# Reordering ScalarE's and VectorE's steps inside the seven-product pairs, and masking attention scores by one more product

## The chip, the cores and the metric

The kernel runs on one core of one Trainium2 chip. The metric is device time: microseconds (us) from the launch to the end on that core, lower is better. TensorE (PE) multiplies, VectorE (DVE), ScalarE (ACT) and GpSimd (POOL) work on tiles in the on-chip memory, SyncE (SP) issues most transfers, and POOL issues those that add into their target.

## What is computed

One inference step of a two-layer encoder for 512 prompt frames and 64 sample frames. The model width is 1024. Layer 0 mixes frames with gated DeltaNet and a short convolution, layer 1 with stick-breaking attention (16 heads of 64); each layer has a SwiGLU feed-forward block (FFN) before and after its mixer. The text counts them in order: FFN 0, mixer 0, FFN 1, FFN 2, mixer 1, FFN 3.

```python
def _swiglu(h, w_in, w_out):                       # D_FF = 2816
    gate, up = jnp.split(h @ w_in, 2, axis=-1)
    return (jax.nn.silu(gate) * up) @ w_out

def _sb_block(q, k, v, q_pos, k_pos):              # stick-breaking attention
    z = jnp.einsum('hqd,hkd->hqk', q, k) * SB_DH ** -0.5
    visible = k_pos[None, :] < q_pos[:, None]
    log_rest = jnp.where(visible, -jax.nn.softplus(z), 0.0)
    later = lax.cumsum(log_rest, axis=2, reverse=True) - log_rest
    w = jnp.where(visible, jnp.exp(jax.nn.log_sigmoid(z) + later), 0.0)
    return jnp.einsum('hqk,hkd->hqd', w, v)

for l in range(DEPTH):                             # DEPTH = 2
    mod = (silu(c) @ ada_w[l] + ada_b[l]) ...      # shift, scale, gate of each sub-layer
    x = x + 0.5 * gate[0] * _swiglu(modulated_norm(x), ff_w_in[l, 0], ff_w_out[l, 0])
    x = x + gate[1] * (delta_and_conv_mixer if l == 0 else stick_breaking_mixer)(modulated_norm(x))
    x = x + 0.5 * gate[2] * _swiglu(modulated_norm(x), ff_w_in[l, 1], ff_w_out[l, 1])
y = _rmsnorm(x, final_g)
```

## The kernel before

All 576 frames are the moving side of every projection, in two halves of 288 columns; weights come in as tiles of 128x128. Every operand is split into a high and a low part (names with H and L, or wh and wl), and one exact product is three matmuls: high by high, low by high, high by low. Such a projection matmul of 288 columns has the tile name `d` as its output, or `a` in one of the seven products, and is called dense below.

The weights are cut into *pairs* of two column tiles, each in two *granules* of 512 KB. `w_dma` (line 370) loads a granule into one of three `stage` buffers. `w_prep` and `w_split` make wh by a copy on ACT and wl by a subtraction on DVE or POOL; where `by_dma` is set (the flag `S2M`, on in FFN 0 to 2), ACT writes the negated high part into wl and a transfer issued on POOL adds the stage tile to it (`acc_dma`).

**Seven-product pairs.** 67 of the input pairs of the four FFNs run through `dense7` (line 514): a 2x2 block product done with seven block products instead of eight, named in the order in which they run P1, P2, P6, P5, P7, P3, P4. Each is 4 blocks of 3 matmuls, so a pair is 84 dense matmuls where a plain one is 96. The weight side needs four sums (`w_sum` 1 to 4, on DVE, tiles `ss`) and four split tiles (`w_tile` 0 to 3). Tile 0 is the stage granule itself, tiles 1 and 2 are sums, and tile 3 is a half tile (`wh3`, `wl3`) that the last product uses. The products share three banks of the accumulation memory: P1, P6, P7 and P4 go through one bank, P5 and P3 through another. So ACT's copy of P1 out of its bank has to be done before P6 may add to it, that of P6 before P7, and so on. `evac7` (line 820) takes the products out: ACT copies (`sg`, `hm`, `up`), DVE sums, and then the split of the result into HH and HL. That last part of a pair (`late`: the product with the gate, HH, HL) runs after the following pair has begun.

**Mixer 1.** Twelve pairs project q, k and v, and the output projection follows. Eight attention tasks (`att_pair`, line 1484; two heads each) are put between the dense matmuls. A task has nine steps. Step i of a task is `scores(i)`: three matmuls of 64 to 512 columns; two sigmoids on ACT (`sg`, `sn`); three operations on POOL that force the last 64 columns of `sg` and `sn` to 0 and 1 where a key is not visible; a running product on DVE from the right (`cp`); a product on DVE (`sg`). Then `transp` turns `sg` round on PE, copies it to `wt`, and after steps 3, 7 and 8 `pv` multiplies it with v. Before its steps a task loads the cached keys and values through SP (`ck`, `vc`) and stores its new k and v the same way.

**Mixer 0** works in the same way with convolutions (`conv_task`, in `raw` buffers handed out by `raw_tile`), small inverses and the recurrence over chunks. **Ada tiles** (`ada_task`) are vector products for shift, scale and gate (`jk<-aw`, two operations on DVE each), spread over the FFNs and mixer 1.

**What sets the order.** The program is unrolled in Python: for each instruction a small model of the engines' clocks (`Model`) adds a cost, and the planner `Sched` decides after each dense block (`S.tick`) whether a task is due. The compiler keeps this order on each engine. So an edit that changes the model's clocks moves instructions elsewhere too. An engine runs its list strictly in order, and SP's loads wait in the list for their buffers.

The evacuation steps of `dense7` are driven by these lines of the main loop:

```python
if n == 0: ... w_tile(i, 3)                       # half tile of this pair, right after P1
k = {0: 0, 3: 1, 5: 2}.get(n)                      # tile 0 after P1, tile 1 after P5, tile 2 after P3
```

Of the kernel before, what the change touches and what calls it, by code (L numbers as in the profile page):

```python
# [303 lines left out]
def encoder_step(ctx: ExitStack, tc: tile.TileContext, a, o):  # L304
# [61 lines left out]
    nxt = [0]  # L366
    share = [False]
# [20 lines left out]

    def w_split(i, src, E=V, by_dma=False):
        n = Model.size(src)  # L390
        if n == HB:
            h, l = (wsp.tile([P, HB], F32R, name=m, bufs=1) for m in ("wh3", "wl3"))
        else:
            h, l = wsp.tile([P, 1024], F32R, name="wh"), wsp.tile([P, 1024], F32R, name="wl")
        wt.setdefault(i, []).append((h, l))
        for c in range(0, n, HB):
            A.activation(h[:, c:c + HB], src[:, c:c + HB], AF.Copy)
        if by_dma:
            A.activation(l[:, :n], src, AF.Copy, scale=-1.0)
            acc_dma(l[:, :n].bitcast(F32), src)  # L400
            return
        E.tensor_sub(l[:, :n], src, h[:, :n].bitcast(F32))

# [16 lines left out]
    def w_tile(i, n):  # L420

        if n == 0:
            w_split(i, st[i, 0], by_dma=S2M[0])
        if n == 1:
            w_split(i, ss[i, 1])
        if n == 2:
            w_split(i, ss.pop((i, 3)))
            ss.pop((i, 1))
            st.pop((i, 0))
            w_dma()  # L430
        if n == 3:
            w_split(i, st[i, 1][:, HB:], by_dma=S2M[0])
            st.pop((i, 1))
            w_dma()

    def w_prep(i, g, E=None):
        if i >= len(pairs) or g >= len(pairs[i]):
            return
        if seven(i):
            if g == 0:  # L440
                w_sum(i, 1)
                w_tile(i, 0)
                w_sum(i, 2)
            else:
                w_sum(i, 3)
                w_tile(i, 1)
# [5 lines left out]
        A.activation(h[:, :n], s[:, :n], AF.Copy)  # L452
        E = E or G if E or share[0] and M.t["POOL"] + 1.1 * n < M.t["DVE"] else V
# [60 lines left out]
    def dense7(evac):  # L514
# [12 lines left out]
        for n, (name, u, xf) in enumerate(order):  # L527
# [15 lines left out]
            if n == 0:  # L543
                if len(wt[i]) < 3:
                    w_sum(i, 4)
                    w_tile(i, 2)
                w_tile(i, 3)
            if nxt7:
                for k in {1: (1,), 2: (2,), 4: (3, 4)}.get(n, ()):
                    w_sum(i + 1, k)  # L550
                k = {0: 0, 3: 1, 5: 2}.get(n)
                if k is not None:
                    w_tile(i + 1, k)
            elif n in (2, 4):
                w_prep(i + 1, n // 2 - 1)
        if not nxt7:
            for n in (0, 1, 2):
# [257 lines left out]
    def ffn(l, s, pool, task, out):  # L815
# [5 lines left out]
        def evac7(jj):  # L821
# [4 lines left out]
            def products(ps):  # L826
                hm = {}

                def mul():
                    for half in (1, 0):  # L830
                        hm[half] = pool.tile([P, 288], F32, name="hm", bufs=2)
                        V.tensor_mul(hm[half], g[half], up[1] if half else ps)

                def high():
                    for half in (1, 0):
                        A.activation(HHc[:, jj, t0s[half]:t0s[half] + 288], hm[half], AF.Copy)

                def low():
                    for half in (1, 0):
                        r = slice(t0s[half], t0s[half] + 288)  # L840
                        V.tensor_sub(HLc[:, jj, r], hm[half], HHc[:, jj, r].bitcast(F32))
                late.update({0: mul, 1: high, 2: low})
# [6 lines left out]
            def evac(step, ps):  # L849
                if step == "P1":  # L850
                    g[0] = copy("sg", ps, 3)
                n = {"P1": 0, "P2": 1, "P6": 2}.get(step, step)
                if step == "P6":
                    g[1] = copy("sg", ps, 3)
                if n in late:
                    late.pop(n)()
                if step == "P2":
                    V.tensor_add(g[0], g[0], ps)
                if step == "P5":
                    up[0] = copy("hm", ps, 2)  # L860
# [11 lines left out]
        for ci, (j0, nj) in enumerate(CHUNKS):  # L872
            HH = pool.tile([P, 8, NT], F32R, name="HH")
            HL = pool.tile([P, 8, NT], F32R, name="HL")
            for jj in range(nj):
                gate = {}

                def evac(g, half, ps, jj=jj, gate=gate):
# [4 lines left out]
                    else:  # L883
                        h = pool.tile([P, 288], F32, name="hm", bufs=2)
# [27 lines left out]
    def mixer0(pool, task, npool):  # L912
# [78 lines left out]
        def conv_task(c, i, raw, out):  # L991
            w = sm["w_qkv"][:, {"q": 0, "k": 4, "v": 8}[c] + i]
            for j in range(4):
# [6 lines left out]
                yield S.clock  # L1000
            yield M.ready(out)
            A.activation(out, out, AF.Silu)

        def raw_tile():
            S.until(lambda: sum(not t[2] for t in convs) < 3)
            return pool.tile([P, RAW], F32, name="raw", bufs=4)
# [66 lines left out]
        def gdn_pair(p, kq, vt):  # L1073
# [50 lines left out]
            for n in range(4):  # L1124
                T.transpose(pv[:, n, :], vt[:, n * P:(n + 1) * P], ident)
# [748 lines left out]
```

## Time and profile before

| what | value |
|---|---|
| median of the runs (lowest to highest) | 2476.76 us (2473.92 to 2480.23) |
| the profiled execution, its own time | 2483.51 us |
| span, first to last instruction | 2481.5 us |
| mean granted clock of TensorE | 0.970 of full speed |
| PE busy | 2353.2 us (95%) |
| DVE busy | 1783.9 us (72%) |
| ACT busy | 1142.1 us (46%) |
| POOL busy | 487.2 us (20%) |
| mean traffic | 133 GB/s |

The busy shares are averages over stages with different limits, and PE's busy time counts overlapping matmuls at their pipelined length. The six stages, in us from the start of the span: FFN 0 0 to 474, mixer 0 to 879, FFN 1 to 1291, FFN 2 to 1701, mixer 1 to 2036, FFN 3 to the end. In the rows below, `a<-b,c` is the tile written and the tiles read, `x` a count, and what stands behind `<-` at an idle time is the engine and tile that ended it.

### The profile page before, as it was taken

What the parts mean: (1) busy time and instruction counts of PE and PEld (TensorE: products, weight loads), DVE (VectorE), ACT (ScalarE), POOL (GpSimd) and SP (SyncE); (2) the same over time, 40 slices, a digit from 0 to 9 for tenths busy, and PEclk for the clock granted to TensorE, in tenths of its full rate; (3) what the DMA queues carried; (4) which work ended last, traced back from release to release, by engine and by line L of the source; (5) the groups of instructions that cost most, each with busy time, mean ns of one, the idle gap of its engine ahead of it and who ended that gap; (6) DMA issues with size and microseconds to landing.
All of it is one profiled execution on the core that took longest, in us unless ns stands there. A gap on an engine that the chain in (4) does not pass through costs nothing. (4 is left out here: it accounts for less than half of the span.)

```text
span 2481.5 us, 46116 instructions
## 1 busy us (share of the span) xinstructions
PE 2353.2 (95%) x18280; PEld 2262.4 (91%) x18280; DVE 1783.9 (72%) x3491; ACT 1142.1 (46%) x2297; POOL 487.2 (20%) x723
## 2 busy tenths in 40 slices
PE   7989899999989999999999999999999979999998
PEld 5989899988878989999999999999888869999998
DVE  7788977587886678686867656466777767848475
ACT  4434626453322355372644446364555445426352
POOL 4100101342231230010132001013443334000001
PEclk9999999998888999999999999999999979999999
DMA  6666757231123156485736556353343315423222
GB/s 242 188 201 191 212 174 179 86 109 53 54 59 98 54 160 189 146 215 160 198 123 179 157 122 159 97 145 100 121 147 115 106 66 140 131 77 102 87 85 82
DMA packets 113115, 329.45 MB, mean 133 GB/s; under 512 B 26706, under 2 KB 29010, under 8 KB 112644
## 3 DMA queue, kind: packets, MB, share of 16 engines
q1 hardware_dynamic: 95044, 273.02, 32.8%
q0 software_dynamic: 17856, 53.49, 12.7%
q8 instruction: 144, 2.36, 0.4%
q14 instruction: 71, 0.58, 0.1%
HBM read 261.47 MB, written 11.51 MB: 110 GB/s over the span
## 5 line engine op out<-in xcount | busy, mean ns | idle before, releaser
L191 PE MATMUL d<-XH,wh 128*128 128x288 f32 x2280 | 702.2, 308 | 17.5 <-ACT XH L191 8.3
L191 PE MATMUL d<-XL,wh 128*128 128x288 f32 x2280 | 687.0, 301 | 15.0 <-POOL XL L191 11.6
L191 PE MATMUL d<-XH,wl 128*128 128x288 f32 x2280 | 686.4, 301 | 9.5 <-DMA wl<-stage 7.9
L191 PEld LDWEIGHTS d<-XH,wh 128*128 128x128 f32 x2280 | 438.8, 192 | 32.2 <-ACT XH L191 14.6
L191 PEld LDWEIGHTS d<-XL,wh 128*128 128x128 f32 x2280 | 439.1, 193 | 22.7 <-POOL XL L191 18.1
L191 PEld LDWEIGHTS d<-XH,wl 128*128 128x128 f32 x2280 | 439.0, 193 | 13.7 <-DMA wl<-stage 11.7
L191 ACT ACTIVATE wh<-stage 128x512 fp32r<-128x512 f32 (+3 forms) x412 | 325.8, 817 | 225.3 <-PE d L191 215.9
L191 PE MATMUL d<-HH,wh 128*128 128x288 f32 x1408 | 416.7, 296 | 1.0 <-ACT HH L191 1.0
L191 PE MATMUL d<-HL,wh 128*128 128x288 f32 x1408 | 416.3, 296 | 0.3
L191 PE MATMUL d<-HH,wl 128*128 128x288 f32 x1408 | 414.2, 294 | 0.0
L191 DVE TENSOR_TENSOR wl<-stage,wh 128x1024 fp32r<-128x1024 f32 (+3 forms) x219 | 246.5, 1133 | 125.6 <-ACT wh L191 123.7
L191 PE MATMUL d<-TH,wh 128*128 128x288 f32 x1072 | 319.9, 298 | 15.3 <-ACT sg L191 12.3
L191 DVE SCALAR_TENSOR_TENSOR jk<-aw,cb 128x1024 fp8e4<-128x1024 f32 x256 | 315.9, 1234 | 4.4
L191 PE MATMUL d<-TL,wh 128*128 128x288 f32 x1072 | 316.3, 295 | 0.0
L191 PE MATMUL d<-TH,wl 128*128 128x288 f32 x1072 | 316.1, 295 | 0.0
L191 DVE SCALAR_TENSOR_TENSOR x<-d,mod,x 128x64 f32<-128x64 f32 (+2 forms) x384 | 146.4, 412 | 225.0 <-PE d L191 224.1
L191 PEld LDWEIGHTS d<-HL,wh 128*128 128x128 f32 x1408 | 264.3, 188 | 1.7 <-DVE HL L191 1.7
L191 PEld LDWEIGHTS d<-HH,wh 128*128 128x128 f32 x1408 | 264.2, 188 | 1.4 <-ACT HH L191 1.4
L191 PEld LDWEIGHTS d<-HH,wl 128*128 128x128 f32 x1408 | 264.6, 188 | 0.0
L563 POOL DMA_DIRECT2D wl<-stage x100 | 86.7, 867 | 847.5 <-ACT wl L191 357.3
L191 ACT ACTIVATE wh<-ss 128x512 fp32r<-128x512 f32 x268 | 158.2, 627 | 153.8 <-DVE ss L191 153.4
L191 PEld LDWEIGHTS d<-TH,wh 128*128 128x128 f32 x1072 | 201.2, 188 | 24.8 <-ACT sg L191 19.7
(325 smaller groups left out, 3796.8 us busy)
## 6 DMA issues: line engine op xcount, KB each, us to landing
stage<-in_w SPq DMA_DIRECT2D x301, 512.0 KB, 3.8
aw<-in_ada SPq DMA_DIRECT2D x128, 512.0 KB, 4.4
wl<-stage POOLq DMA_DIRECT2D x50, 512.0 KB, 5.4
stage<-in_w SPq DMA_DIRECT2D x36, 384.0 KB, 3.1
wl<-stage POOLq DMA_DIRECT2D x50, 256.0 KB, 3.3
TL<-XL POOLq DMA_DIRECT2D x8, 576.0 KB, 8.4
TL<-ss POOLq DMA_DIRECT2D x8, 576.0 KB, 6.7
TL<-in_ada SPq DMA_DIRECT2D x8, 512.0 KB, 7.5
```

The source lines that it names most:

```text
L191: r = real(*args, **kw)
L563: nc.gpsimd.dma_start(out, in_, accum_op=OP.add)
```

## The change

Five edits.

1. **Order inside `dense7`.** wh is made by one ACT copy of 1024 columns instead of two of 512. Making wl is a second step (`rest`) that can be placed apart from wh, and the steps of the next pair's weights are laid out over the seven products. The half tile's wl3 is made by DVE everywhere; before, it came by a transfer in FFN 0 to 2.
2. **The result's split.** `hm` is one buffer of 576 columns (before: two of 288), HH is one ACT copy and HL one DVE subtraction for both halves. They are issued after the third and the fourth product of the following pair instead of the second and the third.
3. **Mixer 1's mask.** The three POOL operations per score are gone. One matmul of 64 columns per score (`hide` by `idR`) adds -1e30 where a key is not visible; both sigmoids then give 0 and 1 there. That is 72 matmuls more and 216 POOL operations fewer.
4. **Mixer 1's weights.** The first granule of ten of its twelve pairs gets wl by the adding transfer: ten more ACT copies and ten more transfers issued on POOL, eleven DVE subtractions of 1024 columns fewer.
5. **Loads and buffers.** One more `w_dma` in the first feed (at `kt == 6`): three stage granules are then on their way at any time, so each later load waits in SP's list for the buffer that was just used. In mixer 0 `raw_tile` also waits until fewer than four `raw` buffers are held.

In all ACT has 307 instructions fewer.

```diff
@@ w_split
-        for c in range(0, n, HB):
-            A.activation(h[:, c:c + HB], src[:, c:c + HB], AF.Copy)
-        if by_dma:
...
+        A.activation(h[:, :n], src, AF.Copy)
+        def rest():
+            if by_dma:
+                A.activation(l[:, :n], src, AF.Copy, scale=-1.0)
+                acc_dma(l[:, :n].bitcast(F32), src)
+            else:
+                E.tensor_sub(l[:, :n], src, h[:, :n].bitcast(F32))
+        return rest
@@ w_prep
+        if g == 0 and pairs[i][g][0][0] == "sb" and pairs[i] != first_sb and pairs[i - 1] != first_sb:
+            A.activation(l[:, :n], s[:, :n], AF.Copy, scale=-1.0)
+            acc_dma(l[:, :n].bitcast(F32), s[:, :n])
+            w_dma()
+            return
@@ dense7, after product n (0 = P1 ... 6 = P4)
-                w_tile(i, 3)
-            if nxt7:
-                for k in {1: (1,), 2: (2,), 4: (3, 4)}.get(n, ()):
-                    w_sum(i + 1, k)
-                k = {0: 0, 3: 1, 5: 2}.get(n)
-                if k is not None:
-                    w_tile(i + 1, k)
...
+                if nxt7:
+                    rest = w_tile(i + 1, 0)
+            if n == 1 and nxt7:
+                rest()
+            evac(n, None)
+            if nxt7 and n in (1, 2):
+                w_sum(i + 1, n)
+            if n == 1:
+                rest = w_tile(i, 3)
+            if n == 3:
+                rest()
+                if nxt7:
+                    w_sum(i + 1, 3)
+            if nxt7 and n == 4:
+                w_sum(i + 1, 4)
+                w_tile(i + 1, 1)()
+            if nxt7 and n == 5:
+                rest = w_tile(i + 1, 2)
+            if nxt7 and n == 6:
+                rest()
@@ evac7
-                        hm[half] = pool.tile([P, 288], F32, name="hm", bufs=2)
...
+                hm = pool.tile([P, NT], F32, name="hm")
...
+                late.update({0: mul, 2: lambda: A.activation(HHc[:, jj], hm, AF.Copy),
+                             3: lambda: V.tensor_sub(HLc[:, jj], hm, HHc[:, jj].bitcast(F32))})
@@ mixer0, raw_tile
-            S.until(lambda: sum(not t[2] for t in convs) < 3)
+            S.until(lambda: sum(not t[2] for t in convs) < 3 and len(holds) < 4)
@@ mixer1
-        V.tensor_scalar(inv, visb, -1.0, 1.0, op0=OP.mult, op1=OP.add)
+        V.tensor_scalar(hide, visb, 1e30, -1e30, op0=OP.mult, op1=OP.add)
@@ scores
+                        if j == 0 and c1 == N:
+                            T.matmul(ps[:, n - 64:n], identR, hide, start=False, stop=False, skip_group_check=True)
-                G.tensor_mul(sg[:, N - 64:N], sg[:, N - 64:N], visb)
-                G.tensor_mul(sn[:, N - 64:N], sn[:, N - 64:N], visb)
-                G.tensor_add(sn[:, N - 64:N], sn[:, N - 64:N], inv)
@@ feed
+            if kt == 6:
+                w_dma()
```

**First place: ACT in a seven-product pair of FFN 0.** Before, from the copy of P1 (`sg<-d`) to the silu of the gate; `wh3` and `wl3` are the half tile's parts, `wh<-stage` and `wl<-stage` tile 0 of the next pair, and the second `sg<-d` is the copy of P6.

```order
L191 ACTIVATE sg_11973<-d_11960 128x288
L191 ACTIVATE wh3_11979<-stage_11838 128x512
L191 ACTIVATE wl3_11980<-stage_11838 128x512
L191 ACTIVATE wh_11986<-stage_11938 128x512 x2
L191 ACTIVATE wl_11987<-stage_11938 128x1024
L191 ACTIVATE HH_11661<-hm_11975 128x288
L191 ACTIVATE HH_11661<-hm_11977 128x288
L191 ACTIVATE sg_12022<-d_11960 128x288
L191 ACTIVATE hm_12040<-d_12027 128x288
L191 ACTIVATE sg_11973<-sg_11973 128x288
```

And now, in a pair of the same chunk.

```order
L191 ACTIVATE sg_11829<-d_11816 128x288
L191 ACTIVATE wh_11831<-stage_11752 128x1024
L191 ACTIVATE wl_11832<-stage_11752 128x1024
L191 ACTIVATE wh3_11854<-stage_11669 128x512
L191 ACTIVATE sg_11869<-d_11816 128x288
L191 ACTIVATE HH_11528<-hm_11812 128x576
L191 ACTIVATE hm_11886<-d_11873 128x288
L191 ACTIVATE sg_11829<-sg_11829 128x288
L191 ACTIVATE up_11907<-d_11816 128x288
L191 ACTIVATE wh_11910<-ss_11852 128x1024
```

Between the copies of P1 and P6 there were seven ACT operations (wh of tile 0 counts as two), and there are three. `wl3` has left ACT, and HH comes after P6's copy as one operation.

**Second place: PE in mixer 1, the second attention task, between its scores of 384 and of 512 keys.** `a<-cm,sg` are the transposes of an earlier step, `kH,qbH` and its two followers the score matmuls, `d<-...` dense matmuls. Before:

```order
L191 MATMUL a<-cm,sg 128x128 x2
L191 MATMUL a<-cm,sg 64x128
L191 MATMUL d<-XH,wh 128x288
L191 MATMUL d<-XL,wh 128x288
L191 MATMUL d<-XH,wl 128x288
L191 MATMUL a<-kH,qbH 128x448
L191 MATMUL a<-kL,qbH 128x448
L191 MATMUL a<-kH,qbL 128x448
L191 MATMUL d<-XH,wh 128x288
L191 MATMUL d<-XL,wh 128x288
L191 MATMUL d<-XH,wl 128x288
```

And now:

```order
L191 MATMUL a<-cm,sg 128x128 x2
L191 MATMUL a<-cm,sg 64x128
L191 MATMUL a<-kH,qbH 128x448
L191 MATMUL a<-hide,idR 128x64
L191 MATMUL a<-kL,qbH 128x448
L191 MATMUL a<-kH,qbL 128x448
L191 MATMUL a<-cm,sg 128x128 x3
L191 MATMUL a<-kH,qbH 128x512
L191 MATMUL a<-hide,idR 128x64
L191 MATMUL a<-kL,qbH 128x512
L191 MATMUL a<-kH,qbL 128x512
```

Before, 3 dense matmuls stood ahead of this score and 15 behind it. Now no dense matmul stands from here to the end of this task's ninth step. The fifth task has none from its score of 448 keys on, the fourth none from 512 on, the third none in its ninth step. In exchange the first task has longer dense runs (96 and 72 in a row) than before.

## Rows read from the trace of the kernel before

**Rows 1.** Windows: us, busy of PE, PEld, DVE, ACT, POOL (instructions); PEclk; DMA.

```profile
474.00:879.00 405.00, 381.24 (x3693) 352.18 (x3692) 305.83 (x801) 143.73 (x281) 118.88 (x201) 0.89 0.24 72
1701.00:2036.10 335.10, 301.76 (x2244) 271.43 (x2242) 252.13 (x512) 173.72 (x410) 134.05 (x263) 0.96 0.35 112
```

**Rows 2.** Windows: two pairs; sums over FFN 0's three chunks and all twelve.

```profile
1486.20:1497.30 11.10, 11.10 (x86) 11.10 (x85) 7.63 (x14) 8.13 (x18) 1.75 (x2) 1.00 0.73 166
...
284.10:297.60 13.50, 12.03 (x87) 11.33 (x86) 12.21 (x23) 8.31 (x17) 1.73 (x2) 1.00 0.83 218
...
sum 206.00, PE 188.04 PEld 181.56 DVE 174.86 ACT 126.73 POOL 26.00; mean PE 62.68 PEld 60.52 DVE 58.29 ACT 42.24 POOL 8.67
...
sum 792.00, PE 764.51 PEld 750.71 DVE 628.76 ACT 505.34 POOL 79.77; mean PE 63.71 PEld 62.56 DVE 52.40 ACT 42.11 POOL 6.65
```

**Rows 3.** Timeline of ACT in one FFN 0 pair: start, us, operation, idle before.

```profile
288.69 0.62 ACT L191 ACTIVATE wl<-stage 128x512 fp32r<-128x512 f32 x1
289.21 1.14 ACT L191 ACTIVATE wh<-stage 128x512 fp32r<-128x512 f32 x2
290.25 1.05 ACT L191 ACTIVATE wl<-stage 128x1024 fp32r<-128x1024 f32 x1
291.50 0.81 ACT L191 ACTIVATE HH<-hm 128x288 fp32r<-128x288 f32 x2 [0.20 <-DVE hm L191]
292.22 0.39 ACT L191 ACTIVATE sg<-d 128x288 f32<-128x288 f32 x1
```

**Rows 4.** What PE waited for, 100 to 440 us: us, times, longest.

```profile
PE d L191 <- ACT sg L191: 7.5, 12, 1.3
PE d L191 <- DMA wl<-stage: 6.1, 5, 4.5
PE d L191 <- ACT hm L191: 3.2, 2, 1.6
```

**Rows 5.** Groups by form: operation and count, busy us, mean ns, idle before.

```profile
L191 DVE TENSOR_TENSOR HL<-hm,HH 128x288 fp32r<-128x288 f32 x176 | 74.9, 457 | 36.9 <-ACT HH L191 35.2
...
L191 DVE TENSOR_TENSOR wl<-stage,wh 128x512 fp32r<-128x512 f32 x17 | 11.7, 688 | 2.7 <-ACT wh L191 2.7
```

**Rows 6.** Waits of PE, then of DVE, in mixer 1.

```profile
PE a L191 <- DVE sg L191: 16.6, 26, 2.5
PE a L191 <- DVE cp L191: 6.5, 7, 2.7
...
DVE cp L191 <- POOL sn L191: 45.4, 46, 2.5
```

**Rows 7.** Timeline at the last attention task's end: sigmoid, last POOL operation, scan.

```profile
2017.40 0.49 ACT L191 ACTIVATE sn<-a 128x384 f32<-128x384 f32 x1
...
2018.36 0.32 POOL L191 TENSOR_TENSOR sn<-sn,inv 128x64 f32<-128x64 f32 x1
...
2018.71 0.96 DVE L191 TENSOR_TENSOR_SCAN cp<-sn,ones 128x384 f32<-128x384 f32 x1 [2.61 <-ACT sg L191]
...
2020.62 0.82 PE L191 MATMUL a<-cm,sg 128*128 128x128 f32 x3 [2.53 <-DVE sg L191]
```

**Rows 8.** Timeline of PE there: two score matmuls of 64 columns.

```profile
2024.49 0.27 PE L191 MATMUL a<-kL,qbH 128*128 128x64 f32 x1
2024.60 0.28 PE L191 MATMUL a<-kH,qbL 128*128 128x64 f32 x1
```

**Rows 9.** Windows: the last attention task's part that has no dense matmuls.

```profile
2003.60:2035.50 31.90, 20.18 (x101) 14.05 (x99) 16.93 (x41) 10.85 (x30) 10.49 (x31) 0.66 0.05 16
```

**Rows 10.** What SP's queue waited for around mixer 1, 1650 to 2036 us.

```profile
SPq L327 <- DVE cp L191: 123.4, 26, 10.4
...
SPq L327 <- DMA wl<-stage: 6.6, 1, 6.6
```

**Rows 11.** Mixer 0, 504 to 879 us: one of PE's waits.

```profile
PE a L191 <- DVE uu L191: 4.0, 4, 1.3
```

**Rows 12.** Windows: a stretch of mixer 0 at the lower clock.

```profile
576.90:590.60 13.70, 13.05 (x179) 10.06 (x183) 9.41 (x32) 1.97 (x4) 2.24 (x7) 0.50 0.27 86
```

More of the change, by code (lines that the diff above doesn't have):

```diff
@@ L366, in encoder_step @@
     nxt = [0]
+    first_sb = [p for p in pairs if p[0][0][0] == "sb"][0]
     share = [False]
@@ L545, in dense7 @@
                     w_sum(i, 4)
-                    w_tile(i, 2)
-                w_tile(i, 3)
-            if nxt7:
-                for k in {1: (1,), 2: (2,), 4: (3, 4)}.get(n, ()):
-                    w_sum(i + 1, k)
-                k = {0: 0, 3: 1, 5: 2}.get(n)
-                if k is not None:
-                    w_tile(i + 1, k)
-            elif n in (2, 4):
+                    w_tile(i, 2)()
+                if nxt7:
[7 more added lines that the diff above has]
+                rest = w_tile(i, 3)
+            if n == 3:
+                rest()
[7 more added lines that the diff above has]
+            if nxt7 and n == 6:
+                rest()
+            if not nxt7 and n in (2, 4):
                 w_prep(i + 1, n // 2 - 1)
         if not nxt7:
-            for n in (0, 1, 2):
+            for n in range(4):
                 evac(n, None)
@@ L849, in evac @@
             def evac(step, ps):
+                if step in late:
+                    late.pop(step)()
                 if step == "P1":
                     g[0] = copy("sg", ps, 3)
-                n = {"P1": 0, "P2": 1, "P6": 2}.get(step, step)
+                if step == "P2":
+                    V.tensor_add(g[0], g[0], ps)
                 if step == "P6":
                     g[1] = copy("sg", ps, 3)
[L855 to L858, printed above, removed]
                 if step == "P5":
-                    up[0] = copy("hm", ps, 2)
+                    up[0] = pool.tile([P, NT], F32, name="hm")[:, :288]
+                    A.activation(up[0], ps, AF.Copy)
                     A.activation(g[0], g[0], AF.Silu)
@@ L883, in evac @@
                     else:
-                        h = pool.tile([P, 288], F32, name="hm", bufs=2)
+                        h = pool.tile([P, 288], F32, name="up") if half else pool.tile([P, NT], F32, name="hm")[:, :288]
                         V.tensor_mul(h, gate[half], ps)
@@ L1000, in conv_task @@
                 yield S.clock
+            give(raw)
             yield M.ready(out)
@@ L1004, in raw_tile, with give @@
         def raw_tile():
-            S.until(lambda: sum(not t[2] for t in convs) < 3)
-            return pool.tile([P, RAW], F32, name="raw", bufs=4)
+            S.until(lambda: sum(not t[2] for t in convs) < 3 and len(holds) < 4)
+            t = pool.tile([P, RAW], F32, name="raw", bufs=4)
+            holds.add(t.tensor.name)
+            return t
+        holds = set()
+        def give(t):
+            holds.discard(t.tensor.name)
         convs = []
@@ L1470, in mixer1 @@
         qbL = pool.tile([P, 9, P], F32R, name="qbL")
-        inv = pool.tile([P, 64], F32, name="inv")
+        identR = pool.tile([P, P], F32R, name="idR")
+        hide = pool.tile([P, 64], F32R, name="hide")
+        A.activation(identR, ident, AF.Copy)
         zf = pool.tile([P, 64], F32, name="zf")
@@ L1744, in feed @@
                 shift(kt + 1)
+            if kt == 6:
+                w_dma()
             if kt == 4:
```

47 lines of the change are left out of this document (21 added, 26 removed).

## The prediction

> **What bounds the kernel now.** I read the windows by stage first, then PE's waits, then timelines. In a seven-product pair the floor is PE: 84 matmuls take 11.1 us when nothing is late, and such a pair exists [rows 2]. The twelve chunks hold 67 of these pairs: 67 x 11.1 = 743.7 us of 792.0 us, so 48 us are above the floor, and 206.0 - 16 x 11.1 = 28 us of them lie in FFN 0 with its 16 pairs [rows 2]. That leaves 20 us for the 51 pairs of the other FFNs. PE's waits in FFN 0 name ACT's copy `sg` (7.5 us), the transfer into wl (6.1 us) and ACT's `hm` [rows 4]. One pair shows why `sg` is late: ACT works from 288.69 to 292.2 us almost without a gap (wl3, wh twice, wl, HH) before it copies P6's bank at 292.22 [rows 3]. But DVE is busy for 12.21 of that pair's 13.50 us [rows 2], so DVE stands close behind. In mixer 1 PE is busy for 301.8 of 335.1 us [rows 1], and what it waits for is the end of an attention step, `sg` and `cp` of DVE, 23.1 us [rows 6]. DVE's scan in turn waits 45.4 us in all for POOL's last mask operation [rows 6]. Mixer 0 has 24 us without PE work [rows 1].
>
> **Seven-product pairs.** Moving HH, wl3 and wl takes ACT's block between P1 and P6 from 0.62 + 0.62 + 1.14 + 1.05 + 0.81 to about 0.62 + 1.05 + 1.05 us (the first 0.62 is wh3, taken equal to wl3; the 1.05 of a 1024-wide copy is that of wl [rows 3]). That is 1.5 us less against P6's waits of at most 1.3 us [rows 4], so these end. wl's transfer is issued earlier and has no half-tile transfer ahead of it, so most of the 6.1 us goes. Against that, wl3 is now DVE's: 0.69 us more per pair in FFN 0 to 2, less about 0.1 for one HL operation in place of two [rows 5]. In the FFN 0 pair shown DVE's 12.21 becomes 12.8 of 13.5 us, so at most 0.7 us comes back there; P1's own `hm` buffer, now single, keeps the `hm` waits (3.2 us) alive [rows 4]. I take 6 of FFN 0's 28 us, and in FFN 1 to 3, where DVE has room, 12 of the 20 us: **-18 us**. Bounds: -32 (14 of 28, since half stays with DVE, and 18 of 20) and -5 (FFN 0 nothing, a quarter elsewhere).
>
> **The mask's product.** 72 matmuls of 64 columns. Two such neighbours start 0.11 us apart [rows 8], so 72 x 0.11 = **+7.9 us**, all on PE, which has no cover.
> [...]
>
> **The end of an attention step.** The 216 POOL operations go. In the dense-free end of the last task, `sn` ends at 2017.89, POOL's last operation at 2018.68 and the scan starts at 2018.71 [rows 7]: 0.8 us per step are saved there. That part takes 31.9 us with PE busy for 20.2 [rows 9], so 11.7 us idle; with 0.8 less on most of nine steps, some 3 to 5 less. What would come next is DVE: scan 0.96 and the product after it. Of the 23.1 us, the part outside the last task, about 12, would go as well if the order stayed: there 15 dense matmuls stand behind a score. It doesn't stay: the second task has none from its score of 384 keys on, the fifth none from 448 on, the fourth none from 512 on. There a wait like the 2.53 us before 2020.62 [rows 7], less 0.8, stands open at each step: ten such steps (four, three, two, and the third task's last) x 1.7 us = +17. Net: 17 - 12 - 4 = +1, and I add 4 because in mid-stage DVE and ACT also carry weight work: **+5 us**, between -15 (bare steps cost nothing, the old waits go) and +15.
>
> **SP's queue.** With three granules always on their way, each load stands in SP's list until its buffer is free, and everything behind it waits too: `aw`, `ck`, `vc`, and mixer 1's outputs. Now ten of mixer 1's granules are released by an adding transfer. SP waited 6.6 us for one of those before mixer 1, and 123.4 us, at no cost to PE that the trace shows, for DVE's `cp` [rows 10]. PE pays where `ck` is late. I take **+4 us**, between 0 and 9 (one such wait and a half).
> [...]
>
> **Clock.** Where PE has only the attention task the granted clock is 0.66 [rows 9], and 0.50 in a stretch of mixer 0 with small matmuls [rows 12]. [...]
>
> **Mixer 0.** Its POOL and ACT work stays, but the planner moves it: at two places `Sb`, `xr` and `uu` (one link of the chunk chain) now follow each other with no dense matmul between, where 12 to 21 stood. PE's waits for `uu` are up to 1.3 us [rows 11]; three links of about 1.2 us at two places give **+7 us**. It can be -3, if the dense matmuls cover other waits, or +17, if a stretch of 14 to 17 us at 0.50 follows as in [rows 12].
>
> What is moved without a price: ACT's 307 fewer instructions elsewhere sit beside PE, which would be late first; in FFN 3 wl3 was DVE's already; ten ACT copies of about 1.05 us in mixer 1 stand on an engine that is busy for 174 of 335 us [rows 1], and lose their cover only beside a bare step, where the 4 us above count them.
>
> **Sum.** -18 + 7.9 + 5 + 4 + 6 + 7 = +12 us. The profiled execution took 2483.5 us and would take 2495.5; it stands 6.7 us above the median of 2476.8, so on that median the forecast is **2489 us**.
>
> **The rivals.**
> - *Forecast: bare attention steps eat the pairs' gain.* 2489 us, its own range 2484 to 2512.
> - *POOL was the whole wait (faster).* If a step without POOL is so short that the transposes of an earlier step and the next score cover it, bare stretches cost nothing. Mixer 1 then gives 7.9 - 15 = -7, SP and clock 0, mixer 0 0: -25, 2452 us. For it: the scan's 45.4 us behind POOL [rows 6]. Against: after `sn` the scan and the product still need some 1.7 us, and a score and a transpose group give 1.0 to 1.9. It decides once a bare step waits less than 0.5 us.
> - *The pairs give back more (no change).* If ACT's block, not DVE, sets FFN 0, the pairs give -30 and the mixers cost 30 as above: 2477 us. For it: 7.5 + 6.1 us of named waits [rows 4]. Against: DVE's 12.21 of 13.5 us.
> - *DVE takes the bound (slower).* wl3 on DVE makes wl of the sums late, and the new order doesn't do what it says: the pairs give -5, the sum is +25, 2502 us.
>
> **How the numbers follow.** A measurement of this kernel can tell about 0.3%, 7.4 us, from no change. Chances: forecast 0.38, DVE 0.10, no change 0.25, POOL 0.27. So slower 0.48, same 0.25, faster 0.27. The range runs from 2460 us (half of the POOL case's chance below) to 2512, the bound of the mixers' terms taken together with a poor gain of the pairs; about 0.2 stay outside.
>
> **What would show it.** Pairs: PE's waits for `sg` in FFN 0 under 2 us, FFN 0's three chunks near 200 us, HL and wl3 at the rows' durations. Mask: 72 matmuls about 0.11 us apart; no POOL in a step; the scan directly behind `sn`. Mixer 1: waits for `sg` of some 1.5 us in the second, fourth and fifth task, with the clock under 1.0 there, and a stage of 350 to 365 us. It is wrong if mixer 1 is at 335 us or less, or if the twelve chunks lose more than 30 us.

## The result, and the profile after

The changed kernel takes 2540.4 us (2536.6 to 2551.7), the kernel before 2478.4 us beside it: a ratio of 1.026, interval 1.022 to 1.030. The forecast was 2489 us with a range of 2460 to 2512. So slower was right, but by 62 us instead of 12, and outside the range. The profiled execution of the changed kernel took 2543.8 us, its span is 2542.1 us: 60.6 us more than the span of before.

Where that went is read from the windows. Below, a *chunk* is a run of two, six or eight seven-product pairs (three chunks in each of the four FFNs, 67 pairs), and a *mixer stretch* reaches from the last chunk before a mixer to the first chunk after it; it holds the mixer, part of its neighbours, and every instruction that the mixer's change moves. The first fence is from the changed kernel: the three chunks of FFN 0, the sum over all twelve chunks, then the stretch of mixer 0 and that of mixer 1. Columns as in [rows 1].

```profile
125.00:168.80 43.80, 30.47 (x169) 29.77 (x170) 37.36 (x60) 15.01 (x26) 1.72 (x2) 0.77 0.53 166
219.70:321.20 101.50, 92.16 (x674) 89.76 (x673) 94.68 (x160) 54.96 (x93) 6.07 (x7) 1.00 0.65 191
373.20:445.90 72.70, 68.12 (x506) 67.18 (x505) 58.32 (x97) 41.32 (x70) 4.34 (x5) 1.00 0.54 153
...
sum 820.10, PE 768.62 PEld 758.34 DVE 661.41 ACT 451.26 POOL 36.50; mean PE 64.05 PEld 63.19 DVE 55.12 ACT 37.61 POOL 3.04
...
445.90:970.40 524.50, 491.49 (x4494) 459.09 (x4493) 374.82 (x940) 194.77 (x373) 151.82 (x238) 0.91 0.29 86
...
1694.60:2190.10 495.50, 452.42 (x3283) 420.55 (x3282) 327.58 (x686) 246.68 (x540) 68.44 (x104) 0.94 0.41 122
```

The same stretch of mixer 1 in the kernel before:

```profile
1660.80:2133.80 473.00, 435.23 (x3210) 402.93 (x3209) 344.06 (x697) 238.18 (x532) 173.82 (x310) 0.96 0.37 115
```

The chunks were 792.0 us in all [rows 2], and now take 820.1: 28 us more, where 18 less were forecast. Mixer 1's stretch takes 22.5 us more and mixer 0's 7.9 more (516.6 before); the rest adds some 2 us. FFN 0's chunks were 206.0 us [rows 2] and are 218.0. In the changed kernel DVE is busy for 37.36 of the first chunk's 43.80 us and for 94.68 of the second's 101.50, while PE is busy for 30.47 and 92.16: no engine is full, so the loss has to be found in what waits for what.

The costliest group of the changed kernel's page names it (group, tiles, count, busy us, mean ns, idle before it, who ended most of that):

```profile
L191 PE MATMUL d<-XH,wh 128*128 128x288 f32 x2280 | 707.8, 310 | 53.5 <-ACT hm L191 36.5
```

Over the whole span PE waited for `hm` for 3.7 us in this group before, and waits 36.5 us now; in FFN 0 alone all its waits for `hm` were 3.2 us in two [rows 4] and are 17.0 us in eleven. Here is one pair of FFN 0's second chunk: PE's, ACT's and DVE's timeline lines that lie around one such wait.

```profile
288.41 0.68 ACT L191 ACTIVATE HH<-hm 128x576 fp32r<-128x576 f32 x1
291.64 0.41 ACT L191 ACTIVATE hm<-d 128x288 f32<-128x288 f32 x1 [2.54 <-DVE HL L191]
...
287.77 1.22 DVE L191 SCALAR_TENSOR_TENSOR jk<-aw,cb 128x1024 fp8e4<-128x1024 f32 x1
289.04 1.23 DVE L191 SCALAR_TENSOR_TENSOR jk<-aw,cb 128x1024 fp8e4<-128x1024 f32 x1
290.19 0.69 DVE L191 TENSOR_TENSOR ss<-ss,stage 128x512 f32<-128x512 f32 x1
290.79 0.75 DVE L191 TENSOR_TENSOR HL<-hm,HH 128x576 fp32r<-128x576 f32 x1
...
292.10 0.40 PE L191 MATMUL d<-XH,wh 128*128 128x288 f32 x1 [1.18 <-ACT hm L191]
```

ACT has made HH by 289.1 us and then stands idle for 2.54 us: the next thing in its list is the copy of P5 into `hm`. That tile is the single buffer that still holds the previous pair's result, and DVE's HL has to read that result first. HL waits on DVE behind an ada tile's two `jk` (1.22 us each) and a weight sum. ACT copies at 291.64, and PE, whose next product in the same bank needs it empty, loses 1.18 us. In the last pair of a chunk a `wl` can stand there instead: in FFN 2, at 1570.59 us, HL follows a `wl` of 1.23 us, and ACT's copy has waited 2.04 us.

In mixer 1, SP's queue waited for the adding transfers ten times (queue, what it waited for, us, times, longest):

```profile
SPq L327 <- DMA wl<-stage: 96.8, 10, 15.0
```

Before, there was one such wait around mixer 1, of 6.6 us [rows 10]. PE's waits for DVE's `sg` in that stretch fell to 8.6 us in 6, where [rows 6] had 16.6 in 26; yet PE's idle time in all rose from 37.8 to 43.1 us, its busy time from 435.23 to 452.42, and the granted clock fell from 0.96 to 0.94.

### The profile page after: what moved, and what is told of

Read it like the earlier page. It is cut to its first block, busy times and chain, and to the rows that moved or that the text cites. A ratio compares the mean times of both kernels' runs of the same rounds, so it can differ in the third digit from the quotient of the medians.

```text
span 2542.1 us, 45405 instructions
## 1 busy us (share of the span) xinstructions
PE 2377.7 (94%) x18352; PEld 2287.6 (90%) x18352; DVE 1789.1 (70%) x3463; ACT 1092.6 (43%) x1990; POOL 340.5 (13%) x468
## 5 line engine op out<-in xcount | busy, mean ns | idle before, releaser
L191 PE MATMUL d<-XH,wh 128*128 128x288 f32 x2280 | 707.8, 310 | 53.5 <-ACT hm L191 36.5
L191 PE MATMUL d<-XL,wh 128*128 128x288 f32 x2280 | 690.9, 303 | 14.5 <-POOL XL L191 11.1
L191 PEld LDWEIGHTS d<-XL,wh 128*128 128x128 f32 x2280 | 443.0, 194 | 22.1 <-POOL XL L191 17.6
L191 ACT ACTIVATE wh<-stage 128x1024 fp32r<-128x1024 f32 (+3 forms) x345 | 319.6, 939 | 224.6 <-PE d L191 207.4
L191 DVE TENSOR_TENSOR wl<-stage,wh 128x1024 fp32r<-128x1024 f32 (+3 forms) x258 | 267.6, 1042 | 133.0 <-ACT wh L191 130.7
L191 DVE SCALAR_TENSOR_TENSOR jk<-aw,cb 128x1024 fp8e4<-128x1024 f32 x256 | 315.5, 1232 | 42.2 <-DMA aw<-in_ada 37.8
L191 PEld LDWEIGHTS d<-TH,wh 128*128 128x128 f32 x1072 | 203.5, 190 | 14.0 <-ACT sg L191 13.8
L191 PEld LDWEIGHTS d<-TH,wl 128*128 128x128 f32 x1072 | 203.6, 190 | 0.1
L191 PEld LDWEIGHTS d<-TL,wh 128*128 128x128 f32 x1072 | 203.5, 190 | 0.0
```

The costliest lines, as they stand in the source:

```text
L191: r = real(*args, **kw)
```

## The experiments

All times are device us; a ratio is to the kernel before, run beside it. In the short diffs, `-` and `+` are against the kernel that the heading names. No run here leaves out any part of the computation. The table gives the stretches that the arguments use; each stretch is read from one profiled execution, while the last line is the median of all runs.

| | before | changed | P5 own | no transfer | both | mask only |
|---|---|---|---|---|---|---|
| FFN 0, chunk of 2 | 32.2 | 43.8 | 40.6 | 43.0 | 40.3 | 32.1 |
| FFN 0, chunk of 8 | 103.0 | 101.5 | 96.8 | 101.5 | 96.7 | 102.9 |
| all 12 chunks | 792.0 | 820.1 | 788.4 | 817.5 | 786.8 | 790.9 |
| mixer 0 stretch | 516.6 | 524.5 | 518.4 | 525.4 | 522.0 | 516.7 |
| mixer 1 stretch | 473.0 | 495.5 | 496.0 | 449.6 | 453.1 | 443.8 |
| median of the runs | 2478.4 | 2540.4 | 2514.4 | 2496.6 | 2469.1 | 2449.4 |

**The changed kernel, with a buffer of its own for P5.** The single `hm` is left to the result, and P5 gets a tile of 288 columns (a table of constants is shortened for room).

```
-                    up[0] = pool.tile([P, NT], F32, name="hm")[:, :288]
+                    up[0] = pool.tile([P, 288], F32, name="p5")
```

> The changed kernel with one edit: ACT's copy of P5 goes into a buffer of its own (p5, 288 columns) instead of the single 576-wide hm, which the previous pair still holds until DVE has made HL. (To make room, the table of constants is 704 columns wide instead of 768; only unused columns are left out.) Theory 'single buffer': PE's waits named ACT hm, 36.5 us over all stages in the changed kernel, go; the twelve chunks of seven-product pairs fall from 820 us to about 788, and the time from 2540 to about 2508 us. Rival 'DVE is the bound': HL, the ada tiles and wl3 fill DVE, so the waits only take another name (ACT sg, wl, HL); the chunks stay above 810 us and the time above 2530.

Measured: 2514.4 us, 1.0175 (1.0138 to 1.0213). Its windows: FFN 0's chunk of eight, and the sum over the twelve.

```profile
218.30:315.10 96.80, 91.64 (x675) 89.74 (x674) 92.47 (x158) 56.45 (x93) 6.06 (x7) 1.00 0.66 196
...
sum 788.40, PE 759.00 PEld 751.98 DVE 656.82 ACT 452.79 POOL 36.41; mean PE 63.25 PEld 62.66 DVE 54.74 ACT 37.73 POOL 3.03
```

The waits for `hm` are gone and the chunks lose 31.7 us: the single buffer was all that the chunks lost, and a little more. But 788.4 is only 3.6 us under the 792.0 of before. In the chunk of eight DVE is now busy for 92.47 of 96.80 us, and PE's floor is 8 x 11.1 [rows 2] = 88.8: DVE is the engine with the least room left there. That it is what holds this chunk is argued from its busy time, not shown.

**The changed kernel, with wl3 by the transfer again.**

```
-            rest = w_split(i, st[i, 1][:, HB:])
+            rest = w_split(i, st[i, 1][:, HB:], by_dma=S2M[0])
```

> The changed kernel with wl3 made by ACT copy and adding transfer again in FFN 0 to 2 (50 half tiles), as in the kernel before. Theory 'single buffer': wl3 stands behind HL in DVE's list, so it does not delay P5's copy in its own pair; ACT gets 0.62 us more per pair; the chunks change by less than 8 us either way and the waits for ACT hm stay above 25 us. Rival 'DVE is the bound': 50 x 0.69 = 34 us of DVE work leave the bound, the chunks of FFN 0 to 2 fall by 15 us or more.

Measured: 2774.2 us, 1.1217 (1.1174 to 1.1261), far from both expectations. PE's waits of this kernel:

```profile
PE d L191 <- DMA wl<-stage: 177.4, 53, 6.4
PE d L191 <- ACT hm L191: 33.4, 25, 3.7
```

The half tile's second step stands after P5 in the changed order; a transfer issued there has not landed (4.4 us for 256 KB in this kernel) when P4, three products on, wants it. All 50 half tiles are late in this way, 169.1 of the 177.4 us; the other three waits are for tile 0. The wait for `hm` stays almost as it was with wl3 off DVE, as the first theory had it. So DVE's load alone doesn't make it, its place in the lists does; and wl3 can't go back to the transfer in this order of steps.

**The changed kernel, without edit 4.** The five lines in `w_prep` are left out, so that all of mixer 1's `wl` are subtractions.

```
-        if g == 0 and pairs[i][g][0][0] == "sb" and pairs[i] != first_sb and pairs[i - 1] != first_sb:
...
-            return
```

> The changed kernel without edit 4: mixer 1's first granules get wl by subtraction on DVE or POOL again, not by the adding transfer. Theory of the prediction 'bare steps': the bare attention steps come from the planner starting attention tasks late, because ck waits in SP's list behind loads that wait for adding transfers; without these, the stretch from FFN 2's last seven-product pair to FFN 3's first falls from 495 us by 10 to 20 us. Rival 'mask product and clock': it falls by less than 5 us, since the 72 products (7.9 us) and the lower clock stay.

Measured: 2496.6 us, 1.0094 (1.0065 to 1.0123). The stretch of mixer 1 in this kernel:

```profile
1693.80:2143.40 449.60, 427.99 (x3282) 401.51 (x3281) 337.30 (x696) 235.14 (x530) 59.61 (x94) 1.00 0.39 122
```

Edit 4 costs 45.9 us in this stretch, far more than expected. PE is busy for 24.4 us less and idle for 21.5 us less (43.1 in the changed kernel, 21.6 here). The busy part is the clock: 1.00 instead of 0.94, with the same matmuls.

**The changed kernel, with POOL's mask back** (edit 3 undone).

```
-                            T.matmul(ps[:, n - 64:n], identR, hide, start=False, stop=False, skip_group_check=True)
...
+                G.tensor_mul(sg[:, N - 64:N], sg[:, N - 64:N], visb)
```

> The changed kernel without edit 3: the three POOL operations mask each score again, the 72 products are gone. Theory of the prediction: bare steps with POOL in the chain are 0.8 us longer each, some ten of them and the nine of the last task, 10 to 15 us, less 7.9 us for the products: the stretch from FFN 2 to FFN 3 (495 us) grows by 2 to 10 us. Rival 'the products cost more than they bring': it falls by 5 to 10 us.

Measured: 2560.2 us, 1.0353 (1.0320 to 1.0386); the stretch of mixer 1 takes 514.2 us, 18.7 more than in the changed kernel. The expectation of 2 to 10 was too low. PE's waits of this kernel in mixer 1:

```profile
PE a L191 <- DVE sg L191: 23.8, 19, 4.6
```

So the mask's product, its own 7.9 us included, gains 18.7 us with edit 4 in place.

**The first and the third together.**

```
-            (five lines of edit 4)
-                    up[0] = pool.tile([P, NT], F32, name="hm")[:, :288]
+                    up[0] = pool.tile([P, 288], F32, name="p5")
```

> The changed kernel with the edits of e1 and e3 together: a buffer of its own for P5's copy, and no adding transfers in mixer 1. If the two losses are independent, 2540 - 26 - 44 gives about 2470 us, at or a little below the kernel before (2473); the twelve chunks near 789 us, the stretch from FFN 2 to FFN 3 near 450 us, which is 23 us under the kernel before. If they feed on each other (a faster pair hands mixer 1 a busier SP queue), the time stays above 2485 us.

Measured: 2469.1 us, 0.9965 (0.9946 to 0.9985). The two gains (26.0 and 43.8 us by the medians) add up to 69.8; 71.4 was measured. (By the ratios 0.85% and 1.66% add up to 2.5%, and 2.95% was measured, which the intervals allow.) They are two separate faults, and without them the change is a gain of about 0.35%.

**The kernel before, with edit 3 alone.** This tells the mask from the rest of the change.

```
+                        if j == 0 and c1 == N:
+                            T.matmul(ps[:, n - 64:n], identR, hide, start=False, stop=False, skip_group_check=True)
...
-                G.tensor_mul(sg[:, N - 64:N], sg[:, N - 64:N], visb)
-                G.tensor_mul(sn[:, N - 64:N], sn[:, N - 64:N], visb)
-                G.tensor_add(sn[:, N - 64:N], sn[:, N - 64:N], inv)
```

> The kernel before with edit 3 alone: the mask as one more product, no POOL operations. Theory 'POOL was the whole wait' (the rival of the prediction): the 23 us that the stretch from FFN 2 to FFN 3 gained in e3 against before are the mask's; 473 falls to about 450 us, the time to about 2452 us. Rival 'bare steps and products eat it' (the prediction's forecast for the mask alone, +7.9 for the products, up to -15 for the waits): the stretch stays above 463 us.

Measured: 2449.4 us, 0.9875 (0.9843 to 0.9907): faster than both kernels, and as the first theory had it. Its stretch of mixer 1, and below it PE's largest waits for the attention steps there:

```profile
1659.20:2103.00 443.80, 428.05 (x3282) 400.63 (x3281) 337.80 (x697) 236.74 (x533) 59.57 (x94) 1.00 0.37 123
```

```profile
PE a L191 <- ACT sn L191: 1.7, 7, 0.2
PE a L191 <- DVE sg L191: 1.0, 2, 0.7
```

The stretch loses 29.2 us, although PE has 72 matmuls more. The waits for `sg` fall from 16.6 us [rows 6] to 1.0, and PE is busy for 7.2 us less, because the clock is 1.00 and not 0.96. The last task now ends while dense matmuls are left, so that the stretch at 0.66 of [rows 9] is gone. PE's list shows it: a score that follows the score of the step before with no dense matmul between them stands there 8 times in the kernel before, all in the last task, and never with the mask alone. This list is not the one of before, since the planner counts the mask too. How much of the 29.2 us is the shorter step itself, and how much the order that the planner makes of it, isn't shown: no run held the order fixed for the mask. The kernel with both faults removed takes 17.6 us more by its span: 4 less in the chunks, 5 and 9 more in the two mixer stretches, and 7 more in the plain pairs between the chunks.

The price of one product is seen at a score of 512 keys. Before, the first and the third matmul of such a score:

```profile
1794.88 0.40 PE L191 MATMUL a<-kH,qbH 128*128 128x512 f32 x1
...
1795.34 0.40 PE L191 MATMUL a<-kH,qbL 128*128 128x512 f32 x1
```

And with the mask's product among them:

```profile
1818.66 0.40 PE L191 MATMUL a<-kH,qbH 128*128 128x512 f32 x1
1818.89 0.19 PE L191 MATMUL a<-hide,idR 128*128 128x64 f32 x1
1818.92 0.47 PE L191 MATMUL a<-kL,qbH 128*128 128x512 f32 x1
1819.23 0.40 PE L191 MATMUL a<-kH,qbL 128*128 128x512 f32 x1
```

First to last start is 0.46 us before and 0.57 now: 0.11 us for the product, as [rows 8] had it.

**The changed kernel's transfers in the order of the kernel without them.** Two kernels part edit 4 into what its transfers do and what the planner's new clocks do. In the first the transfers are made, but the planner counts subtractions, so that PE's and SP's lists are those of the kernel without edit 4.

```
-            A.activation(l[:, :n], s[:, :n], AF.Copy, scale=-1.0)
-            acc_dma(l[:, :n].bitcast(F32), s[:, :n])
+            nc.scalar.activation(l[:, :n], s[:, :n], AF.Copy, scale=-1.0)
+            nc.gpsimd.dma_start(l[:, :n].bitcast(F32), s[:, :n], accum_op=OP.add)
+            M.issue(E.name, [l[:, :n]], [s[:, :n], hb], E.cost("tensor_sub", ...))
```

> The changed kernel with its ten adding transfers in mixer 1, but with the planner's clocks kept as if they were subtractions, so that PE and SP have the order of e3 word for word. Theory 'order' (the prediction's: attention steps laid bare by the planner cost the time): within 10 us of e3 (2497), below 2507. Rival 'queue' (each transfer really holds its stage buffer and everything behind it on SP): 2525 or more, as in the changed kernel.

Measured: 2512.7 us, 1.0133 (1.0102 to 1.0164), between the two expectations.

```profile
1697.10:2165.00 467.90, 439.91 (x3282) 410.83 (x3281) 325.94 (x686) 244.43 (x540) 68.28 (x104) 0.97 0.43 129
```

**Subtractions in the changed kernel's order.** The other way round: DVE subtracts, and the planner counts the transfers.

```
-            A.activation(l[:, :n], s[:, :n], AF.Copy, scale=-1.0)
-            acc_dma(l[:, :n].bitcast(F32), s[:, :n])
+            nc.vector.tensor_sub(l[:, :n], s[:, :n], h[:, :n].bitcast(F32))
+            (the planner's clocks of the copy and the transfer)
```

> The mirror of e7: PE and SP in the changed kernel's order word for word (the planner's clocks count the ten adding transfers), but DVE makes these ten wl by subtraction, no transfer runs. Theory 'order': stays at 2525 us or more. Rival 'queue': falls below 2510 us.

Measured: 2530.9 us, 1.0219 (1.0185 to 1.0253), as the theory 'order' had it.

```profile
1697.80:2190.10 492.30, 454.42 (x3282) 420.47 (x3281) 337.47 (x694) 236.41 (x529) 59.56 (x94) 0.93 0.35 111
```

| mixer 1 stretch | subtraction | transfer |
|---|---|---|
| order without edit 4 | 449.6 | 467.9 |
| order with edit 4 | 492.3 | 495.5 |

By these stretches the order alone costs 27.6 to 42.7 us, the transfers themselves 18.3 in the good order and 3.2 in the bad one. But a stretch is one execution, and the one behind 492.3 is the slowest of its kernel's four, 14.9 us above their median. By the ratios of all runs (1.0094 and 1.0133, 1.0219 and 1.026) the order costs some 31 us with either way of making wl, and the transfers some 10 us in either order, which the intervals don't tell from nothing. That the transfers' price depends on the order isn't shown.

That most of edit 4's cost is not in any transfer, but in the planner's reading of them, holds by both. PE's lists show what the order does: the scores with no dense matmul before them, as counted above, are 14 in the changed kernel and 5 without edit 4. The likely way there is read from the kernel's text and not tested: in the model a later `wl` frees its stage buffer later, so later loads, `ck` among them, count as late, tasks are put off, and their steps are left without dense matmuls between them.

**The mask alone, with P5's own buffer and an earlier HH.** From the kernel with the mask only: HH after P6's copy and HL after P5, two of the pair's moves without the reordered weights.

```
+                n = {"P1": 0, "P6": 1, "P5": 2}.get(step, step if step == 0 or ps is None else None)
...
-                    up[0] = copy("hm", ps, 2)
+                    up[0] = copy("p5", ps, 1)
```

> The kernel of e6 (before with the mask as a product), and in the seven-product pairs two edits alone: P5's copy in a buffer of its own, and HH after P6's copy, HL after P5; the weights' steps stay where the kernel before has them. Theory 'ACT block': HH (0.81 us) no longer stands before P6's copy, so PE's waits for ACT sg (12.5 us in e6) fall by half or more and the waits for hm (3.4) go: the chunks fall from 791 to about 782, the time from 2449 to about 2441 us. Rival 'DVE is the bound in FFN 0': FFN 0's chunks stay within 3 us and the whole within 4 us of e6.

Measured: 2451.5 us, 0.9907 (0.9881 to 0.9933): no gain over the mask alone. Over the whole span PE's waits for `sg` fall from 12.5 to 5.3 us and those for the transfer into `wl` rise from 8.6 to 13.8. In the profiled execution, which is 8.7 us above the median, the chunks give 3 us and the plain pairs between them take 11. What the first chunk lost in the changed kernel isn't seen here (31.3 us), so it belongs to something that this kernel doesn't have: the weights' side of edit 1, the joined HH and HL, or the extra load of edit 5.

**The mask alone, with the wait of `raw_tile`.** From the kernel with the mask only: the last part of edit 5, to see mixer 0.

```
-            S.until(lambda: sum(not t[2] for t in convs) < 3)
+            S.until(lambda: sum(not t[2] for t in convs) < 3 and len(holds) < 4)
```

> The kernel of e6 with one more part of the change: raw_tile of mixer 0 also waits until fewer than four raw buffers are held. Theory 'holds': the 8 us that mixer 0's stretch (FFN 0's last seven-product pair to FFN 1's first) took longer in the changed kernel come from this wait: 516.7 becomes about 524 us, the time about 2457. Rival 'moved by the pairs': mixer 0 got longer because FFN 0's new pairs shift the planner's clocks; the stretch stays within 3 us of 516.7.

Measured: 2454.3 us, 0.9909 (0.9872 to 0.9945); the stretch of mixer 0 takes 514.9 us, against 516.7 without the wait. So on its own this wait doesn't make mixer 0's 8 us. Taking it out of the changed kernel wasn't tried.

**Both faults removed, with wl3 on POOL.** From the kernel with both faults removed: does DVE's load set FFN 0?

```
-            rest = w_split(i, st[i, 1][:, HB:])
+            rest = w_split(i, st[i, 1][:, HB:], G)
```

> The kernel of e5 with wl3 (all 67 half tiles) subtracted by POOL instead of DVE, at the same place in the pair. In e5 DVE is busy for 95% of FFN 0's second chunk. Theory 'DVE is the next bound' (the prediction's last rival, for what is left once the hm wait is gone): 0.69 us per pair leave DVE, PE's waits for ACT sg and DVE wl (26.9 us in e5) fall by 10 us or more, FFN 0's three chunks (206.6 us in e5) fall by 6 us or more. Rival 'order of ACT and DVE, not load': they stay within 3 us; or POOL's slower subtraction makes P4 wait for wl in each pair and they grow.

Measured: 2479.5 us, 1.0019 (1.0000 to 1.0039), 10 us slower than with wl3 on DVE. FFN 0's chunks take 214.1 us instead of 206.5, and PE's waits for `sg` in FFN 0 rise from 11.6 to 19.8. One group of DVE by form, first with wl3 on DVE:

```profile
L191 DVE TENSOR_TENSOR ss<-stage 128x512 f32<-128x512 f32 x134 | 91.9, 686 | 7.9 <-DMA stage<-in_w 7.8
```

and with wl3 on POOL, with POOL's own group:

```profile
L191 DVE TENSOR_TENSOR ss<-stage 128x512 f32<-128x512 f32 x134 | 110.3, 823 | 4.5 <-DMA stage<-in_w 4.4
...
L191 POOL TENSOR_TENSOR wl<-stage,wh 128x512 fp32r<-128x512 f32 x67 | 106.3, 1586 | 351.9 <-ACT wh L191 351.9
```

The mean of 823 ns is made of two kinds: 118 of the 134 sums ran clear of POOL's subtraction and took 682 ns, the 16 that met one took 1864. One such meeting in FFN 0, of DVE and then of POOL; the first line's operation takes 0.45 us elsewhere:

```profile
246.81 2.14 DVE L191 TENSOR_TENSOR hm<-sg,up 128x288 f32<-128x288 f32 x1
248.87 0.44 DVE L191 TENSOR_TENSOR hm<-sg,d 128x288 f32<-128x288 f32 x1
...
247.03 1.60 POOL L191 TENSOR_TENSOR wl<-stage,wh 128x512 fp32r<-128x512 f32 x1
```

So the load did not leave DVE: in FFN 0's chunks it is busy for 195 us instead of 186, with 16 subtractions fewer. This run can't say what FFN 0 would take with a lighter DVE; that stays open.

Not every DVE operation was longer beside POOL's subtraction: `hm<-sg,up`, with both inputs in the on-chip memory, took 1536 ns on average in the 11 cases that met one and 451 in the other 56, while `hm<-sg,d`, with one input in the accumulation memory, took 443 in the four that met one and 446 elsewhere. Why the two differ is not shown.

## Why the prediction was wrong, step by step

**The pairs: -18 forecast, +28 measured.** The step that failed is the sentence "P1's own `hm` buffer, now single, keeps the `hm` waits (3.2 us) alive". (The product that is copied into it is P5; the text named the wrong one.) The single buffer was seen, its waits were priced as before, and the pair's gain was summed as if ACT's block alone mattered. What it does is new: it ties ACT's copy of P5 to DVE's HL of the previous pair, which edit 2 also put one product later. In the whole span 36.5 us of PE's idle time answer to it, 17.0 of them in FFN 0 where 3.2 were expected to stay, and P5's own buffer gives 31.7 us back in the chunks. The prediction costed the buffer by the rows of before, where two buffers left that wait open only twice in FFN 0; the right price was to follow the two lists: what stands on DVE ahead of HL ([rows 3] shows the copies, the timeline of DVE would have shown `jk`, 1.2 us twice).

What was expected of ACT's block did not come either. In the changed kernel the waits for `sg` in FFN 0 (from 100 us to its last chunk's end) are three of 6.1 us in all, one of them 5.0, in place of twelve of 7.5 [rows 4]; but with the buffer repaired they are seven of 10.6, and five for DVE's `wl`, 5.3 us, come in addition. The chunks are then 3.6 us shorter than before, not 18, the least that the term's bounds allowed being 5. DVE got no lighter: HL's 0.75 us in place of 2 x 0.457 [rows 5] saves DVE 0.16 us in a pair, and wl3 costs it 0.69. The rival "DVE takes the bound" had the right engine, and it was given 0.10.

FFN 0's first chunk is still 8 us longer after the repair (40.6 against 32.2). DVE is busy there for 35.5 us instead of 27.7: three `TL` of 1.35 us (part of the sums on the frames' side) and one more ada tile's two `jk`, which stood ahead of the chunk before, now fall into it, and two wl3. DVE reaches them later: the second `TL` starts at 117.2 us before and at 123.0 in the changed kernel, where up to 125 us DVE's `jk` waited 7.7 us for the ada tile's data `aw`, and not at all before. The prediction's section on SP's queue had named this wait and priced it in mixer 1 alone. SP's list before and now:

```profile
72.67 1.46 SPq L327 DMA_DIRECT2D stage<-in_w  x2
74.19 0.42 SPq L327 DMA_DIRECT2D aw<-in_ada  x1
...
71.87 8.52 SPq L327 DMA_DIRECT2D stage<-in_w  x3
80.44 0.42 SPq L327 DMA_DIRECT2D aw<-in_ada  x1
```

The third load is the one that edit 5 adds, and `aw` stands behind it and is issued 6.3 us later. No run leaves that load out, so that it makes what the first chunk loses is likely, but not shown.

**The mask's product: +7.9 forecast, right.** 0.11 us: with the mask alone, from 64 to 512 keys the median from first to last start grows by 0.11 us, at 64 from 0.14 to 0.25. (In the changed kernel it grows by 0.10 to 0.12 us up to 448 keys, and by 0.19 at 512.)

**The end of a step: +5 forecast.** The term added new bare steps, +17, and took away two waits. The mask alone goes the way of the rival "POOL was the whole wait", and further: -29.2 us in the stretch where that rival had -7, since time at the half clock went as well (PE busy 7.2 us less in spite of 7.9 us more work). The bare steps that were counted in the changed order are there, but they come from edit 4, not from the mask: without edit 4 the stretch takes 449.6 us with the mask in place. What failed here was to read the bare steps of the changed order as the mask's consequence, when two edits had moved that planner. The mask is worth 18.7 us in the changed order and 29.2 in the order of before.

**SP's queue: +4 forecast, 46 measured for edit 4.** The step "one such wait and a half" took the wait of 6.6 us [rows 10] as one of a kind. There are ten, 9.7 us each. Even that is the smaller part: with the order held fixed, the transfers cost 18 us or 3 by the stretches and some 10 by the ratios. The larger part, 28 to 43 us by the stretches and some 31 by the ratios, is the order that the planner makes of them, which the prediction had under "the end of an attention step".

**Clock: +6 forecast.** No run shows this term by itself; what the runs show is the granted clock. Read by the microsecond it is 1.00 or 0.50: of 31 whole microseconds in the stretch of [rows 9], 18 show 0.50, 8 show 1.00, and the 5 others, where it changes, a value between; [rows 12] is at 0.50 throughout. A mean of 0.96 over 473.0 us is then an estimated 2 x 0.04 x 473.0 = 38 us at half speed, a mean of 0.94 over 495.5 is 59 us: 21 us more at half speed are some 10 us of PE's work, and PE's busy time did rise by 17.2 us, 7.9 of them the mask's. So 6 us was of the right size, by the bare steps that were named; without edit 4, which makes them, the clock is 1.00.

**Mixer 0: +7 forecast, +7.9 measured.** The size is right in part by luck, and the reason isn't right. The waits for `uu` fell (4.0 us in [rows 11], 2.3 now); another wait grew, from 2.9 us to this line of the changed kernel:

```profile
PE a L191 <- DVE ot L191: 11.3, 2, 6.2
```

The raw buffers' wait alone doesn't make it. The list of PE in this stretch is the same in the changed kernel, with P5's own buffer, without edit 4, with both, and in the two kernels that part edit 4: it took 524.5, 518.4, 525.4, 522.0, 527.3 and 528.7 us. So one list gives from 2 to 12 us more than the 516.6 of before, and +7.9 is one draw of these. Which edit makes that list no run shows.

**The sum.** The mixers were forecast at +30 (7.9 + 5 + 4 + 6 + 7) and came out at +30.4 (22.5 + 7.9). That agreement is a cancellation: the mask alone is -29.2, edit 4 +45.9, the other edits +5.8 in mixer 1 (449.6 less 443.8) and +7.9 in mixer 0. By the spans the prediction's error is 60.6 - 12 = 48.6 us; 46 of them are the pairs'.

## What to carry to other kernels

When a step is joined or moved, follow each of its buffers to its last reader, and look at what stands in that reader's list ahead of it; the waits that a trace of before shows for a buffer say nothing about the same buffer made single. When a planner driven by a cost model sets the order, an edit's own price and the price of the order that it provokes are two terms: hold the order fixed once and the edit once, as the four kernels on mixer 1 do for edit 4, and compare medians of several runs, not one profiled execution. And of a change in several parts, run each part alone: here one edit is worth 1.2%, and the others together cost three times that.

## What the runs showed of the hardware that was not expected

- A subtraction moved from DVE to POOL cost DVE more than it saved in FFN 0: a sum `ss` that met one of POOL's subtractions (1586 ns on average) took 1864 ns instead of 682, and DVE's busy time rose from 186 to 195 us.
- With the mask alone, a 64-column product squeezed in between the matmuls of a score costs 0.11 us at every score's width from 64 to 512 keys, though at 512 keys its own start lies only 0.03 us ahead of its follower's.
- In mixer 1 the clock did more than its waits: from the kernel without edit 4 to the changed one, the mean granted clock falls from 1.00 to 0.94, PE's busy time rises from 427.99 to 452.42 us for the same number of matmuls, and its idle time by 21.5 us.
